# First-level products of the chunked recurrence scheduled six ticks behind their operands instead of three

## The chip, the cores and the metric

The kernel runs on one core of a Trainium2 chip. The metric is the device time of one execution in microseconds (us); lower is better. The engines are named as the profile names them: PE multiplies matrices, DVE works on vectors and reads the matmul results, ACT applies functions and copies, POOL adds and issues some transfers, SP issues most transfers.

## The reference

One layer of a hybrid encoder over 2048 rows of width 1024, in fp32. The part that the change touches is the gated linear recurrence (4 heads of 128), written chunk by chunk:

```python
def hgrn2_mixer(zq, zf, zi, zo, lb, norm_g):
    q = jax.nn.silu(heads(zq))
    f = lbh + (1.0 - lbh) * jax.nn.sigmoid(heads(zf))
    log_f = jnp.log(f)
    k = 1.0 - f
    v = heads(zi)
    ...
    def step(state, xs):
        qc, kc, vc, gc = xs
        b = jnp.cumsum(gc, axis=2)
        diff = b[:, :, :, None, :] - b[:, :, None, :, :]
        decay = jnp.exp(jnp.where(causal[:, :, None], diff, -jnp.inf))
        attn = jnp.einsum('bhtk,bhtsk,bhsk->bhts', qc, decay, kc)
        o = (jnp.einsum('bhts,bhsv->bhtv', attn, vc)
             + jnp.einsum('bhtk,bhkv->bhtv', qc * jnp.exp(b), state))
        ...
def reference(...):
    for l in range(DEPTH):
        xn = rmsnorm(x, norm1_g[l])
        z = xn @ w_in[l]
        ...
        ya = pool_mixer(u_pool, pool_w[l], pool_scale[l]) @ w_pa[l]
        yb = hgrn2_mixer(zq, zf, zi, zo, lower_bounds[l], hgrn_norm_g[l]) @ w_pb[l]
        merged = gates[:, :, 0] * ya + gates[:, :, 1] * yb
        x = x + merged @ w_o[l]
        x = x + conv_glu_ffn(rmsnorm(x, norm2_g[l]), w_up[l], conv_w[l], conv_b[l], w_down[l])
    return rmsnorm(x, final_g)
```

## The kernel before

**Tiling.** The rows go through in two passes of 1024, each of two halves of 512 columns (rows lie on the free axis). A pass is a mixer (the input projection, the pooling branch, the recurrence, two branch projections `pa` and `pb`, the output projection `wo`) and then a feed-forward part (`up`, `dn`). Each big product is made as seven block products, P1 to P7, by a scheme of the Strassen kind, over sums of blocks (`B11`, `T1`, ...), and each block product as three matmuls per tile, because an fp32 operand is split in a high and a low part (`ops`, lines 212 and 213 for the weights). A unit of the projection is 7 x 12 = 84 matmuls of 128x512, all recorded on line 147. The first pass also writes the sums of weight blocks that it makes (line 411) to DRAM (`kw...`, line 321), for the second pass.

**What sets the order.** The program is written as tasks (Python generators) that are stepped between matmuls. `mm` records one big matmul; every sixth is a *tick* (`MM_PER_TICK`), on which the next weights are converted and every task whose wait is over is stepped; `yield n` in a task means n ticks, which is 6n big matmuls. From this recording, a scheduler gives each engine a fixed order. A call of `in_turn(ins)` keeps the instruction behind the last big matmul recorded before it; all else may be moved. Each engine runs its own order strictly: an instruction that waits holds what is queued behind it on that engine.

**The recurrence.** `hgrn_task` runs for one head and one half of the rows; the projection units `fr` (forget logits and q), `ur` (pooling input) and `gr` (gates) are what the PE does meanwhile. When a unit `fr` is done, its two halves are queued, and two tasks run side by side. A task makes the 128x128 matrices of attention weights (`att`, shown as `at`) level by level, for pairs of blocks of 1, 2, 4 and 8, 16 and 32, and 64 rows. A level's product on PE (`pl`, lines 986, 946, 999) needs `ks` (k) and a form of q from DVE and ACT; DVE then copies the product into `att` under masks (lines 993, 1006, 954, 957) and multiplies decay into q, k and d (f) for the next level (lines 1012, 1014, 1016, 967 and others). After the levels come a transposition of k (`pk`), the state update (`pv` on PE, line 1029; `ss`, four steps on DVE, line 1037), the output (`po`, lines 1045 and 1047), its norm (ACT line 1052, POOL 649 and 650, DVE `ot` 1058) and a transposition (`pt`, line 1064).

The operands of the first level are q1, made on ACT (lines 903, 904) and DVE (line 905), and k (line 894). Between them and the product stands the `yield 3` on line 908. The other levels wait `AHEAD`, which is 3, in the same place.

**Buffers.** Nearly every 128x512 tile lies in one of 77 shared slots (`N_SLOTS`). A new tile takes a slot that an old one leaves; if the old one was being stored to DRAM, the first writer of the new tile waits for that store to land. Which slot a tile gets is settled with the order. The pooling branch (`pool_task`, sums `s` on line 854, `p` on line 859, `pm` on lines 867 to 869) and the gates (`gt`, line 1354, stored by line 876) draw on the same slots.

Of the kernel before, what the change touches and what calls it, by code (L numbers as in the profile page):

```python
# [70 lines left out]
AHEAD = 3  # L71
# [9 lines left out]
def tile_trunk(  # L81
# [803 lines left out]
    def hgrn_task(b, h, d, q, vd, zd, od):  # L885
# [19 lines left out]
        dve.tensor_tensor(q1[:, :, 0], qo, do, ALU.mult)  # L905
        dve.tensor_tensor(qe, qe, de, ALU.mult)
        dve.tensor_tensor(qo, q1[:, :, 0], de, ALU.mult)
        yield 3
        def mask(key, n):
            m = masks[key]  # L910
            return m.unsqueeze(1).to_broadcast([P, n, m.shape[1], m.shape[2]])
# [365 lines left out]
    def mixer(b0, forms, late):  # L1277
# [14 lines left out]
        def runner():  # L1292
            while taken[0] < 2 * HEADS:
                if queue:
                    taken[0] += 1
                    yield from hgrn_task(*queue.pop(0))
                else:
                    yield 1
# [487 lines left out]
```

## Time and profile before

| | us |
|---|---|
| median of 3 runs | 2555.31 |
| lowest, highest | 2554.01, 2557.34 |
| the profiled execution's own time | 2554.45 |
| its span (first to last instruction) | 2552.7 |
| PE idle over the span | 34.1 |
| of it before products of line 986, waiting for line 905 | 5.2 |

The page gives busy time by engine; PE idle is the span less its 2518.6 us busy. A timeline row has the start, the length, the engine, the line, the operation and the tiles; the bracket at its end is the idle time of the engine just before it and what ended that. A matmul of 128x512 is listed with about 0.4 us but the next starts 0.23 us after it, since they overlap. "PEclk" is the granted clock of PE as a share of full speed.

### The profile page before, as it was taken

To read this page: it belongs to the slowest core of one execution; us is meant where nothing else is said; L and a number is where in the kernel's file an instruction comes from. 1 tells how busy PE (TensorE), PEld (TensorE's weight loads), DVE (VectorE), ACT (ScalarE), POOL (GpSimd) and SP (SyncE) were. 2 spreads that over 40 slices of the span, in tenths; PEclk is the share of its full clock that TensorE was granted. 3 is DMA by queue.
4 is the path that set the end of the run, shared out by engine and by line. 5 is a ranking of instruction groups with operands and counts; after the bars stand their busy time and mean duration, and the time that the engine had idled before them with its cause. 6 is when DMAs were issued, how large, how long until landed. Compare 5 with 4: busy or idle time off the path is not lost.

```text
span 2552.7 us, 35665 instructions
## 1 busy us (share of the span) xinstructions
PE 2518.6 (99%) x11508; PEld 2058.3 (81%) x11508; DVE 1978.0 (77%) x3518; ACT 1176.0 (46%) x2218; POOL 753.4 (30%) x1117
## 2 busy tenths in 40 slices
PE   9999999999999999999999999999999999999998
PEld 7788877888788888888887888888887888888887
DVE  7798869588888787885585877675978888778755
ACT  6434434324545454554454343432355554545534
POOL 1344344002454334461230111200034433325410
PEclk9999999999999999999999999999999999999999
DMA  7777767768898879997444343446443544446952
GB/s 261 236 196 228 212 182 230 238 214 240 194 248 247 226 223 246 258 356 254 134 147 149 102 134 112 132 153 221 149 159 96 157 150 144 148 137 231 332 162 100
DMA packets 252332, 493.76 MB, mean 193 GB/s; under 512 B 26544, under 2 KB 43056, under 8 KB 251824
## 3 DMA queue, kind: packets, MB, share of 16 engines
q1 hardware_dynamic: 185664, 315.70, 39.2%
q0 software_dynamic: 41504, 110.64, 16.9%
q10 hardware_dynamic: 24976, 65.13, 7.4%
q8 instruction: 91, 1.49, 0.2%
q14 instruction: 97, 0.79, 0.1%
HBM read 381.79 MB, written 187.17 MB: 223 GB/s over the span
## 4 chain that ended last, share of the span: by engine, by line
PE 71%; DVE 1%; ACT 1%; issue 0%; POOL 0%; POOLq 0%; DVEq 0%; ACTq 0%
PE dn_P L147 16%; PE up_Z L147 14%; PE up_V L147 9%; PE up_X L147 9%; PE wo_P L147 3%; PE gr_Z L147 3%; PE gr_X L147 2%; PE pb L147 2%; PE gr_V L147 2%; PE pa L147 2%; PE fr_Z L147 1%; PE io_Z L147 1%; PE fr_X L147 1%; PE io_V L147 1%; PE fr_V L147 1%; PE pl L946 1%
## 5 line engine op out<-in xcount | busy, mean ns | idle before, releaser
L212 ACT CAST ops<-raw 128x512 fp32r<-128x512 f32 x736 | 454.3, 620 | 835.7 <-PE dn_P L147 176.2
L213 DVE TENSOR_TENSOR ops<-raw,ops 128x512 fp32r<-128x512 f32 x736 | 548.8, 749 | 208.3 <-ACT ops L212 203.0
L1522 DVE SCALAR_TENSOR_TENSOR e<-h,cols,e 128x512 f32<-128x512 f32 x176 | 143.1, 816 | 31.7 <-ACT e L1520 23.3
L1520 ACT ACTIVATE e<-h,cols 128x512 f32<-128x512 f32 x176 | 142.6, 814 | 24.9 <-DVE h L1079 18.6
L1525 DVE SCALAR_TENSOR_TENSOR e<-h,cols,e 128x512 f32<-128x512 f32 x176 | 134.0, 770 | 2.8
L881 POOL DMA_DIRECT2D g_P<-dg_P x154 | 85.1, 560 | 161.0 <-PE dn_P L147 116.0
L1186 POOL TENSOR_TENSOR gf_P<-e,e 128x512 f32<-128x512 f32 x44 | 61.1, 1389 | 149.2 <-DVE e L1531 95.7
L1317 POOL TENSOR_TENSOR q<-q,qs 128x512 f32<-128x512 f32 x16 | 21.8, 1364 | 199.5 <-ACT qs L1316 192.3
L1186 POOL TENSOR_TENSOR gf_P<-gf_P,e 128x512 f32<-128x512 f32 x44 | 59.2, 1345 | 72.2 <-DVE e L1531 71.7
L1515 POOL COPY h<-h 128x2 f32<-128x2 f32 x88 | 42.0, 489 | 114.0 <-DVE h L1078 109.9
L1529 ACT ACTIVATE e<-e 128x512 f32<-128x512 f32 x88 | 55.5, 631 | 38.6 <-DVE e L1525 38.3
L1517 POOL COPY hist<-h 128x2 f32<-128x2 f32 x88 | 36.0, 409 | 117.8 <-DVE h L1079 116.1
L1079 DVE TENSOR_TENSOR h<-up_u,up_V 128x512 f32<-128x512 f32 x88 | 60.1, 683 | 13.4 <-PE up_V L147 12.9
L1354 ACT ACTIVATE gt<-gt,cols 128x512 f32<-128x512 f32 x48 | 34.8, 725 | 75.9 <-DVE gt L1079 47.6
L1161 DVE TENSOR_TENSOR x<-x,wo_P 128x512 f32<-128x512 f32 x88 | 56.0, 681 | 12.2 <-PE wo_P L147 12.0
L1161 DVE TENSOR_TENSOR ac<-ac,dn_P 128x512 f32<-128x512 f32 x72 | 47.1, 682 | 16.5 <-PE dn_P L147 16.4
L1545 POOL DMA_DIRECT2D dg_P<-gf_P x88 | 51.4, 584 | 7.9 <-POOL gf_P L1186 7.2
L931 POOL COPY qm<-q 128x64 f32<-128x64 f32 x64 | 23.0, 377 | 100.7 <-DVE q L937 34.8
L1113 ACT COPY up_e<-up_X 128x512 f32<-128x512 f32 x44 | 25.8, 587 | 57.8 <-PE up_X L147 52.7
L946 PE MATMUL pl<-qm,k 128*128 128x192 f32 x256 | 50.3, 326 | 0.3 <-DVE qm L935 0.3
L1515 POOL COPY h<-hist 128x2 f32<-128x2 f32 x88 | 46.1, 531 | 7.7 <-DVE m_T42l L618 7.7
L946 PEld LDWEIGHTS pl<-qm,k 128*128 128x128 f32 x256 | 44.2, 189 | 5.1 <-issue 0.6
(1301 smaller groups left out, 8118.1 us busy)
## 6 DMA issues: line engine op xcount, KB each, us to landing
g_P<-dg_P POOLq DMA_DIRECT2D x154, 256.0 KB, 6.1
raw<-in_w_up_t SPq DMA_DIRECT2D x132, 256.0 KB, 3.1
raw<-in_w_in_t SPq DMA_DIRECT2D x98, 256.0 KB, 3.4
dg_P<-gf_P POOLq DMA_DIRECT2D x88, 256.0 KB, 4.0
dg_P<-e SPq DMA_DIRECT2D x66, 256.0 KB, 3.4
raw<-in_w_dn SPq DMA_DIRECT2D x66, 256.0 KB, 3.8
x<-in_x SPq DMA_DIRECT2D x64, 256.0 KB, 4.8
gd<-gt ACTq DMA_DIRECT2D x64, 256.0 KB, 3.6
```

What stands on the lines that cost most here:

```text
L147: count[1] = pe.matmul(*args, **kw)
L212: self.mark = act.copy(hi, v)
L213: low = self.low = dve.tensor_tensor(lo, v, f32(hi), ALU.subtract)
L881: eng.dma_start(t, d)
L946: ins = pe.matmul(pa_[:, c * 192 : c * 192 + 192], ks[:, (i + c) * P : (i + c + 1) * P], mv[:, c].rearrange("p s x -> p (s x)"), start=Tru ...
L1079: return dve.tensor_tensor(dst, t, ps, ALU.add if how == "add" else ALU.subtract)
L1161: dve.tensor_tensor(t, t, ps[j], ALU.add if sg > 0 else ALU.subtract)
L1186: pin(eng.tensor_tensor(t, x0, x1, op))
L1515: pool.tensor_copy(h[:, 0:2], hist[:, mt] if hf == 0 else hs[s, 0][:, TB : TB + 2])
L1520: in_turn(act.activation(t, h[:, 2:], AF.Identity, bias=col(o_cb + mt), scale=col(o_cw + 4 * MF + mt)))
L1522: in_turn(second(dve.scalar_tensor_tensor(t, h[:, 1 : 1 + TB], col(o_cw + 2 * MF + mt), t, ALU.mult, ALU.add)))
L1525: dve.scalar_tensor_tensor(t, h[:, 0:TB], col(o_cw + mt), t, ALU.mult, ALU.add)
```

## The change

The first level's products are recorded six ticks (36 big matmuls) behind their operands, where it was three (18). Every other wait keeps its number, and nothing else is edited; so all later steps of each task are recorded later too.

```diff
@@ -905,7 +905,7 @@
         dve.tensor_tensor(q1[:, :, 0], qo, do, ALU.mult)
         dve.tensor_tensor(qe, qe, de, ALU.mult)
         dve.tensor_tensor(qo, q1[:, :, 0], de, ALU.mult)
-        yield 3
+        yield 2 * AHEAD
         def mask(key, n):
             m = masks[key]
             return m.unsqueeze(1).to_broadcast([P, n, m.shape[1], m.shape[2]])
```

Every engine has the same instructions before and after; they are in another order, and tiles lie in other slots, in the two mixers alone.

**PE, the first pair of tasks of the first pass.** Before (`q_0_1492` and `q_0_1506` are the two halves' q1; the rows left out are the other big matmuls of the same units):

```order
L147 MATMUL gr_0_Z<-x_T23l,ops_1415 128x512
L147 MATMUL gr_0_Z<-x_T23h,ops_1415 128x512
L986 MATMUL pl_0_1_1539<-q_0_1492,k_0_1487 128x128 x4
L147 MATMUL gr_0_X<-x_f4h,ops_1481 128x512
...
L147 MATMUL gr_0_X<-x_f7h,ops_1481 128x512
L986 MATMUL pl_0_1_1544<-q_0_1506,k_0_1501 128x128 x4
L147 MATMUL gr_0_V<-x_T10h,ops_1434 128x512
```

And now:

```order
L147 MATMUL gr_0_Z<-x_T23h,ops_1415 128x512
L147 MATMUL gr_0_V<-x_T10h,ops_1434 128x512
...
L147 MATMUL gr_0_X<-x_f7h,ops_1481 128x512
L147 MATMUL gr_0_Z<-x_T30h,ops_1457 128x512
...
L986 MATMUL pl_0_1_1574<-q_0_1492,k_0_1487 128x128 x4
L986 MATMUL pl_0_1_1579<-q_0_1506,k_0_1501 128x128 x4
L147 MATMUL gr_0_Z<-x_T32h,ops_1457 128x512
...
L147 MATMUL gr_0_Z<-x_T43h,ops_1528 128x512
L986 MATMUL pl_0_2_1648<-q_0_1493,k_0_1487 128x128 x4
L986 MATMUL pl_0_2_1653<-q_0_1507,k_0_1501 128x128 x4
```

The first half's product stands 30 big matmuls later and the second's 18; both are at one place now, and the second level's products follow 18 big matmuls behind them, where it was 36 and 24. The same holds for the last pair of the first pass (30 later, second level 18 behind, before 24 and 36) and for these pairs of the second pass.

**DVE, behind the first state update of the first pass.** A bracket names the semaphores that the instruction waits for; DMAHW ones are those of transfers. Before:

```order
L1115 TENSOR_TENSOR fr_1_u_2063<-fr_1_e_2035,fr_1_Z 128x512 [waits DVE_49,PE_49]
L854 TENSOR_TENSOR s_1_2_2080<-s_1_1_1985 128x512 [waits DMAHW7_49,DMAHW1_49,Pool_49]
L1037 SCALAR_TENSOR_TENSOR ss_0_2095<-st_0_122,f_0_1424,pv_0_2090 128x128 [waits DMAHW7_49,PE_49]
L213 TENSOR_TENSOR ops_2075<-w56s_2072,ops_2075 128x512 [waits Activation_49]
L859 SCALAR_TENSOR_TENSOR p_0_2110<-s_0_1_2009,u_0_1993 128x512 [waits DVE_49]
```

And now:

```order
L213 TENSOR_TENSOR ops_2061<-w56s_2058,ops_2061 128x512 [waits Activation_49]
L213 TENSOR_TENSOR ops_2095<-raw_1732,ops_2095 128x512 [waits DMAHW1_49,Activation_49]
L854 TENSOR_TENSOR s_1_2_2080<-s_1_1_1977 128x512 [waits DMAHW7_49,DVE_49]
L859 SCALAR_TENSOR_TENSOR p_0_2098<-s_0_1_2009,u_0_1985 128x512 [waits DVE_49]
L618 TENSOR_TENSOR pl_0l<-p_0_2098,pl_0h 128x512 [waits DMAHW0_49,Activation_49]
L854 TENSOR_TENSOR s_1_2_2104<-s_1_1_2013 128x512 [waits PE_49]
L1119 TENSOR_TENSOR fr_1_u_2113<-fr_1_Z,fr_1_e_2021 128x512 [waits DVE_49]
L1079 TENSOR_TENSOR q_1_2115<-fr_1_u_2113,fr_1_V 128x512 [waits DVE_49,PE_49]
L1037 SCALAR_TENSOR_TENSOR ss_0_2142<-st_0_122,f_0_1424,pv_0_2137 128x128 [waits PE_49]
```

Before, the pooling sum `s_1_2` of line 854 took slots whose stores (DMAHW7, DMAHW1) had been issued 142 and 55 big matmuls earlier, and the state step followed at once. Now it takes the slot of `w56s`, a weight sum whose store to `kwfq1ins` (DMAHW7) is issued at the same place of the order; the state step stands six instructions behind it, and PE needs that step 27 big matmuls behind the `pv` products.

**DVE, the third head's state update in the first pass.** Before:

```order
L854 TENSOR_TENSOR s_3_2_3705<-s_3_1_3612 128x524 [waits DVE_49,PE_49]
L213 TENSOR_TENSOR ops_3732<-raw_3320,ops_3732 128x512 [waits DMAHW1_49,Activation_49]
L1037 SCALAR_TENSOR_TENSOR ss_2_3720<-st_0_126,f_2_2994,pv_2_3715 128x128 [waits DMAHW3_49,DVE_49]
L1037 SCALAR_TENSOR_TENSOR ss_2_3720<-ss_2_3720,f_2_2994,pv_2_3715 128x128 [waits DVE_49] x2
L1037 SCALAR_TENSOR_TENSOR st_1_127<-ss_2_3720,f_2_2994,pv_2_3715 128x128 [waits DVE_49]
```

And now:

```order
L854 TENSOR_TENSOR s_3_2_3694<-s_3_1_3586 128x524 [waits DMAHW2_49,DVE_49]
L854 TENSOR_TENSOR s_3_2_3718<-s_3_1_3627 128x524 [waits Pool_49]
L1119 TENSOR_TENSOR gr_4_u_3727<-gr_4_Z,gr_4_e_3643 128x512 [waits DVE_49,PE_49]
L1079 TENSOR_TENSOR gt_1_4_3729<-gr_4_u_3727,gr_4_V 128x512 [waits DMAHW3_49,DVE_49,PE_49]
L213 TENSOR_TENSOR ops_3746<-w100s_3743,ops_3746 128x512 [waits Activation_49]
L213 TENSOR_TENSOR ops_3781<-w100s_3740,ops_3781 128x512 [waits Activation_49]
L1037 SCALAR_TENSOR_TENSOR ss_2_3756<-st_0_126,f_2_2969,pv_2_3751 128x128 [waits DMAHW5_49,DVE_49,PE_49]
```

The state step now takes the slot of `w100s`, whose sum POOL makes once PE has passed the second half's `pk`, and whose store to `kwfq3ins` follows that sum; the products `po` that need the step stand 36 big matmuls behind that `pk`.

## The prediction

> **What bounds the kernel now.** I read the page first.
>
> ```profile
> span 2552.7 us, 35665 instructions
> ...
> PE 2518.6 (99%) x11508; PEld 2058.3 (81%) x11508; DVE 1978.0 (77%) x3518; ACT 1176.0 (46%) x2218; POOL 753.4 (30%) x1117
> ...
> PE 71%; DVE 1%; ACT 1%; issue 0%; POOL 0%; POOLq 0%; DVEq 0%; ACTq 0%
> ```
>
> PE is busy for 2518.6 of 2552.7 us, and the chain that ended last is PE for 71% and hardly anything else. So PE's own work sets the time, and a change that leaves every matmul in place can only alter what PE loses between them: 2552.7 - 2518.6 = 34.1 us. The list of who waited for whom on PE says what these are (total, times, longest):
>
> ```profile
> engine line waited for: us in total, times, longest us
> PE pl L986 <- DVE q L905: 5.2, 3, 2.3
> ...
> PE pt L1064 <- DVE ot L1058: 2.5, 2, 1.8
> PE gr_X L147 <- ACT gr_e L1113: 2.2, 2, 1.6
> ...
> PE pl L999 <- DVE k L967: 1.4, 2, 0.9
> PE pm L867 <- ACT pl_2h L617: 1.2, 1, 1.2
> ```
>
> The wait that the change is about is the first: 5.2 us in three waits for line 905, which makes q1. The other rows shown are waits inside the mixers, for steps that the change moves. The busy time by stretch shows where there is anything to lose (each engine's busy time with its count, then clock, DMA share and GB/s):
>
> ```profile
> core 0: us, PE busy (x) PEld busy (x) DVE busy (x) ACT busy (x) POOL busy (x), PEclk, DMA share, GB/s
> 110.00:560.00 450.00, 439.56 (x2148) 363.82 (x2147) 352.57 (x776) 161.42 (x358) 145.45 (x153) 0.99 0.74 216
> ...
> 1290.00:1720.00 430.00, 427.01 (x2131) 356.31 (x2130) 325.87 (x772) 188.12 (x401) 66.41 (x104) 1.00 0.44 133
> ```
>
> In the first mixer (110 to 560 us) PE is idle for 450.0 - 439.6 = 10.4 us, DVE is busy for 78% and the DMA engines for 74%; in the second (1290 to 1720 us) PE is idle for 3.0 us and the DMA share is 44%. What a moved step may newly run into is therefore in the first mixer.
>
> **Term 1, the three waits for line 905: -5.2 us.** The first of them, and DVE's row at it:
>
> ```profile
> 128.11 0.40 PE L147 MATMUL gr_Z<-x_T23h,ops 128*128 128x512 f32 x1
> 130.18 1.13 PE L986 MATMUL pl<-q,k 128*128 128x128 f32 x8 [1.67 <-DVE q L905]
> ...
> 131.38 0.39 PE L147 MATMUL gr_X<-x_f4l,ops 128*128 128x512 f32 x1
> ...
> 133.69 0.40 PE L147 MATMUL gr_X<-x_f7h,ops 128*128 128x512 f32 x1
> ```
>
> ```profile
> 129.62 0.41 DVE L905 TENSOR_TENSOR q<-q,f 128x256 f32<-128x256 f32 x1
> ...
> 131.42 0.41 DVE L905 TENSOR_TENSOR q<-q,f 128x256 f32<-128x256 f32 x1
> ```
>
> PE was free at 128.11 + 0.40 = 128.51 (by the pace of its matmuls at 128.34) and q1 of the first half was there at 129.62 + 0.41 = 130.03. From 131.38 to 133.69 ten matmuls start, so one costs 0.231 us. The product now comes 30 matmuls later: 128.34 + 30 x 0.231 = 135.3 us, 5.2 us after q1 of the first half and 3.5 us after that of the second (131.83). The same distance of 30 is there at the other two waits:
>
> ```profile
> 140.40 1.95 PE L986 MATMUL pl<-q,k 128*128 128x128 f32 x16
> ...
> 142.88 0.39 PE L147 MATMUL gr_Z<-x_T41h,ops 128*128 128x512 f32 x1
> ...
> 394.26 3.24 PE L986 MATMUL pl<-q,k 128*128 128x128 f32 x16 [2.29 <-DVE q L905]
> ...
> 398.43 0.39 PE L147 MATMUL gr_V<-x_T11h,ops 128*128 128x512 f32 x1
> ```
>
> ```profile
> 1401.03 1.13 PE L986 MATMUL pl<-q,k 128*128 128x128 f32 x8 [1.24 <-DVE q L905]
> 1403.80 0.50 PE L147 MATMUL gr_X<-x_f4h,ops 128*128 128x512 f32 x1 [1.64 <-ACT gr_e L1113]
> ```
>
> The waits there are 2.29 and 1.24 us; 30 matmuls are 6.9 us, so both vanish. 1.67 + 2.29 + 1.24 = 5.2 us. At 1403.80 a wait of 1.64 us for ACT's copy of the unit's first product (gr_e) follows. In the new order 12 other matmuls (2.8 us) stand ahead of that row in place of the wait and the product (1.24 + 0.8 us), but ACT's queue has one more conversion ahead of the copy; I leave the 1.64 us as it is.
>
> **Term 2, the clock behind the longest of them: -1.7 us.** The 16 products and three matmuls from 140.40 to 142.88 took 2.48 us. The same work from 394.26 to 398.43, behind the wait of 2.29 us, took 4.17 us. The difference is 1.69 us, and the stretch around it shows why:
>
> ```profile
> 391.00:398.00 7.00, 4.71 (x23) 4.12 (x22) 7.00 (x14) 5.10 (x12) 3.66 (x4) 0.77 0.99 265
> ```
>
> The granted clock was 0.77 there, against 0.99 over the mixer. Behind 1.67 us of waiting there is no such loss (131.38 to 133.69 is the usual pace). So the 2.29 us wait cost some 4 us, and this goes with it. [...]
>
> **Term 3, the third of the kind, k for the 64-row level: -1.4 us.**
>
> ```profile
> 433.62 0.65 PE L999 MATMUL pl<-q,k 128*64 128x64 f32 x8 [0.94 <-DVE k L967]
> ```
>
> This wait (0.94, and 0.4 for the other half; 1.4 in the list) comes 14 matmuls behind the 16-row products. In the new order the distance is 23, so PE arrives 9 x 0.231 = 2.1 us later on this clock, and 0.94 us is covered.
>
> **Term 4, the waits behind one held slot: -3.0 us.** In the first pass one stall of DVE is a slot whose store had not landed:
>
> ```profile
> 363.79 0.70 DVE L854 TENSOR_TENSOR s<-s 128x520 f32<-128x520 f32 x1 [4.90 <-DMA gd<-gt]
> ```
>
> ```profile
> 366.99 0.30 PE L1064 MATMUL pt<-ident,ot 128*128 128x128 f32 x1 [1.80 <-DVE ot L1058]
> ...
> 371.62 0.50 PE L867 MATMUL pm<-pl_2h,ops 128*128 128x512 f32 x1 [1.22 <-ACT pl_2h L617]
> ```
>
> DVE stood for 4.9 us at a pooling sum, what is queued behind it came late, and PE waited 1.80 us for the output of the third head and 1.22 us for a pooled half. In the new order that sum takes another slot and these two products stand 24 and 12 matmuls later (5.5 and 2.8 us), so I take both waits out.
>
> **Term 5, what the new slots cost: +5 us, between 0 and 10.5.** Slots are dealt anew, and two places look tight. How long a store takes is in the rows of the first mixer (count, KB, median us to landing), and in one row of ACT:
>
> ```profile
> gd<-gt ACTq DMA_DIRECT2D x32, 256.0 KB, 3.7
> ...
> kwfq3ins<-w100s SPq DMA_DIRECT2D x2, 256.0 KB, 9.0
> ...
> kwfq1ins<-w56s SPq DMA_DIRECT2D x1, 256.0 KB, 11.7
> ```
>
> ```profile
> 187.63 0.86 SPq L321 DMA_DIRECT2D kwfq1ins<-w56s  x1
> ...
> 199.44 0.69 ACT L871 ACTIVATE mx<-pm,cols 128x512 f32<-128x512 f32 x1 [6.34 <-DMA kwfq1ins<-w56s]
> ```
>
> The rows at the place of need and at the weight sum, from before:
>
> ```profile
> 184.66 1.63 POOL L411 TENSOR_TENSOR w56s<-w51s,raw 128x512 f32<-128x512 f32 x1 [5.25 <-ACT pl_0h L617]
> ...
> 199.06 0.39 PE L147 MATMUL fr_V<-x_B223h,ops 128*128 128x512 f32 x1
> ```
>
> Place B: DVE's pooling sum now waits for the store of w56s. Before, that store was issued at 187.63 and held ACT until 199.44. Less the 1.67 us gained by then it lands at 197.7; the sum and five more DVE operations of some 0.6 us stand ahead of the state step, which is then there at 197.7 + 3.7 = 201.4. The matmul of the second row is the one that stands at the need in the new order, 27 behind `pv`; PE came to it at 199.06, and now comes 1.67 us of waiting and some 0.8 us of small products sooner, at about 196.5. That is a wait of 4.9 us at most. But POOL's sum, which stood 5.25 us behind ACT's copy of `pl_0h`, waits for PE's `pk` alone in the new order, so the store may go out some 5 us sooner, and then the wait is 0. Place C: the state step of the third head waits for the store of w100s, 9.0 us, behind such a POOL sum (1.6 us), which starts only when PE is 36 matmuls (8.3 us) ahead of the need. With 0.3 us for the first step that is 1.6 + 9.0 + 0.3 - 8.3 = 2.6 us at most, and 0 if the store lands as quickly as the gates' (3.7 us). Elsewhere I allow what the one held slot of before cost, 0 to 3.0 us. Together 0 to 10.5; the rows lie on both sides of the middle, so I take 5. Below nothing it cannot be, since these waits were not there.
>
> What the change costs beside that: the second level's products now follow 18 matmuls (4.2 us) behind the first level's. In between DVE must copy and multiply k for both halves:
>
> ```profile
> L1006 DVE COPY_PREDICATED at<-m,pl 128x256 f32<-128x256 uint8 x32 | 24.5, 767 | 0.0
> ...
> L1014 DVE TENSOR_TENSOR k<-k,f 128x256 f32<-128x256 f32 x48 | 24.0, 500 | 0.0
> ...
> L993 DVE COPY_PREDICATED at<-md,pl 128x256 f32<-128x256 uint8 x32 | 23.5, 735 | 3.0 <-PE pl L986 3.0
> ```
>
> That is 2 x (0.74 + 0.77 + 0.50) = 4.0 us at these lengths. With the other half's eight product instructions (0.8 us) PE has 5.0 us of other work; I cost it at nothing, and it is a rival below. The tail is covered too: the last head's output comes 24 matmuls later, some 100 matmuls ahead of the first `pb` product.
>
> **The sum.** -5.2 - 1.7 - 1.4 - 3.0 + 5.0 = -6.3 us. On the profiled execution's 2554.45 us that is 2548.2; the median shown, 2555.31, lies 0.9 us above it, so 2549.0 us.
>
> **The rivals.** (1) *Slot holds win, slower.* The mechanism is term 5 alone: a held DVE instruction in the first pass makes PE wait for over 2 us, and each such wait takes the clock with it, 1.7 us as at 394.26. B at 4.9 + 1.7, C at 2.6 + 1.7 and 3.0 elsewhere are 13.9 us against gains of 11.3: 2557.9 us; with one more hold as long as the 4.9 us one and not covered by PE's work, 4.9 + 1.7 more: 2564.5. It decides from 11.3 us on. For it: a DMA share of 74%, stores of 9.0 and 11.7 us, and stores issued just ahead of their wait. Against it: 36 matmuls of cover at C, the earlier sum at B. (2) *The next level takes the wait.* DVE is held between the levels, as the 1.64 us and the 4.9 us rows show can be, and the second level's products wait up to 1.5 us at four places, 6 us: -6.3 + 6 gives 2555.0 us, no change; with half of it, 2552. For it: 18 matmuls in place of 24 to 36. Against: in the list of before PE never waited for line 1014 or 1006, at distances of 24 and more. (3) *All moved waits vanish and none comes*, -11.3: 2544.0 us. (4) *The change doesn't do what it says*, the scheduler having put the products back: 2555.3; the order of PE speaks against it.
>
> **How the numbers follow.** Forecast 0.45, around 2549 with a range of its own from 2545.5 to 2551.5. Slot holds 0.20, next level 0.19, all gains 0.13, nothing moved 0.03. A measurement of this kernel tells about 0.2%, 5.1 us, from no change: below 2550.2 is faster, above 2560.4 slower. Faster: 0.39 of the forecast's 0.45 and the 0.13, 0.52. Same: 0.06 of the forecast, the 0.19, 0.03 and 0.06 of the slot holds, 0.34. Slower: 0.14. For 8 in 10 the range leaves out the lower end of "all gains" and the slot holds above 2558: 2543 to 2558 us.
>
> **What would show it.** Right: no row "pl L986 <- q L905" among PE's waits, no clock of 0.77 in the first mixer, and a PE idle time of the second mixer of under 2 us. Term 5 shows as idle time of PE before `po` (line 1047) with a transfer as the cause on DVE. Wrong: a wait of PE at line 986 for k (line 1014) is rival 2; several waits over 2 us in the first mixer, each with a lower clock behind it, are rival 1. Idle time or clock lost outside the two mixers would make the whole account wrong, since nothing moves there.

## The result, and the profile after

| | before | after |
|---|---|---|
| median of 5 runs (us) | 2554.01 | 2567.69 |
| lowest, highest | 2550.76, 2557.34 | 2566.11, 2568.71 |
| span of the profiled execution | 2552.7 | 2566.0 |
| PE busy, PE idle in it | 2518.6, 34.1 | 2522.4, 43.6 |

The changed kernel takes 1.0055 times as long, with an interval from 1.0045 to 1.0066: slower by some 14 us, where 6.3 us less were forecast (2549.0 us) and at most 2558 us were allowed for. The page of the changed kernel, span and busy times:

```profile
span 2566.0 us, 35639 instructions
...
PE 2522.4 (98%) x11508; PEld 2058.8 (80%) x11508; DVE 1980.7 (77%) x3518; ACT 1177.3 (46%) x2218; POOL 741.2 (29%) x1117
```

The span grew by 13.3 us: 9.5 us are more idle time of PE (43.6 - 34.1), and 3.8 us are more busy time for the same instructions, which goes with a lower mean granted clock of PE (0.995 for 0.997). The list of PE's waits after the change (total, times, longest) shows what came and what went:

```profile
engine line waited for: us in total, times, longest us
PE gr_Z L147 <- DVE gr_u L1119: 10.3, 6, 3.5
PE gr_X L147 <- ACT gr_e L1113: 3.9, 2, 2.0
...
PE pv L1029 <- ACT kt L1022: 2.6, 1, 2.6
...
PE pt L1064 <- DVE ot L1058: 2.4, 1, 2.4
```

The waits for line 905 (5.2 us in three), for line 967 (1.4) and for `pl_2h` (1.2) are no longer in the list. In their place stands one that hardly was there before (0.5 us in two): PE waits in front of `gr_Z` for DVE's `gr_u`, line 1119, 10.3 us in six waits. Four of them are at the pairs (3.50, 1.59, 1.52 and 1.50 us), one of 1.75 us is at the second head. And it waits 2.6 us for `kt` and 2.4 us for the last `ot`.

To see where the 13.3 us lie I cut both executions at places up to which PE has run the same set of instructions, and compared the pieces (from the starts of PE's rows, times of before in brackets):

| piece of the program | before | after | difference |
|---|---|---|---|
| ahead of the first recurrence products (to 126) | 124.4 | 123.3 | -1.1 |
| first pair, to the products of the 4-row level (to 148) | 21.7 | 26.6 | +4.9 |
| from there (to 265) | 117.6 | 117.6 | -0.1 |
| from there (to 350) | 84.8 | 86.0 | +1.2 |
| third head's state update (to 391) | 41.2 | 42.9 | +1.7 |
| last pair (to 472) | 80.8 | 79.1 | -1.8 |
| first `pa` products (to 488) | 16.0 | 22.2 | +6.2 |
| second mixer, first pair (1396 to 1418) | 21.8 | 23.8 | +2.0 |
| second mixer, last pair (1652 to 1673) | 20.9 | 22.8 | +1.9 |
| the rest (to 2540) | 2009.3 | 2007.6 | -1.7 |

Three things carry the loss: three of the four pairs (the last pair of the first pass gained 1.8 us), the stretch of the `pa` products, and the third head's state update. One execution of each kernel is compared, and a piece differs by 1 to 2 us between executions with the same order in it: in the kernel `tail_pin` of experiment 6, which has the changed kernel's order up to the `pa` products, the first pair lost 3.9 us and the third head's state update 0.3 us.

**The pairs.** PE's and then DVE's rows at the first pair after the change:

```profile
134.63 1.95 PE L986 MATMUL pl<-q,k 128*128 128x128 f32 x16
...
141.48 0.80 PE L147 MATMUL gr_Z<-x_T40h,ops 128*128 128x512 f32 x1 [3.50 <-DVE gr_u L1119]
```

```profile
137.85 0.71 DVE L993 COPY_PREDICATED at<-md,pl 128x256 f32<-128x256 uint8 x1
138.37 0.76 DVE L1006 COPY_PREDICATED at<-m,pl 128x256 f32<-128x256 uint8 x1
138.93 0.45 DVE L1014 TENSOR_TENSOR k<-k,f 128x256 f32<-128x256 f32 x1
...
140.75 0.67 DVE L1119 TENSOR_TENSOR gr_u<-gr_Z,gr_e 128x512 f32<-128x512 f32 x1
```

The 16 first-level products of both halves now run at 134.63, six big matmuls ahead of the point where PE begins the next block product in bank `gr_Z` (a bank, in the kernel, is the place in which PE leaves a product until another engine has read it). Before PE may write that bank again, DVE must have read it; that read is line 1119, called u3 below. But in DVE's order the six instructions that work on the products (lines 993, 1006, 1014, twice; the second three are left out above) stand ahead of line 1119. DVE gets to it at 140.75, so PE waits 3.50 us. Before the change the same two instructions were here:

```profile
140.60 0.69 DVE L1119 TENSOR_TENSOR gr_u<-gr_Z,gr_e 128x512 f32<-128x512 f32 x1
```

```profile
142.10 0.47 PE L147 MATMUL gr_Z<-x_T40h,ops 128*128 128x512 f32 x1
```

DVE came to line 1119 at about the same time, 140.60, but PE only asked for it at 142.10: it had waited 1.67 us earlier and had 16 products of the second level (1.95 us) between the two block products. The change took the earlier wait away, moved these products behind the bank's turn, and so turned both into a later, longer wait. What it cost beyond its length is in the windows (the clock is the third figure from the end):

```profile
core 0: us, PE busy (x) PEld busy (x) DVE busy (x) ACT busy (x) POOL busy (x), PEclk, DMA share, GB/s
...
141.40:144.90 3.50, 3.42 (x8) 2.75 (x9) 0.71 (x2) 2.33 (x6) 0.41 (x2) 0.50 0.19 75
144.90:149.90 5.00, 5.00 (x27) 4.30 (x27) 2.90 (x6) 1.04 (x3) 2.14 (x3) 0.78 0.12 45
```

The granted clock was 0.50 for 3.5 us and 0.78 for the next 5 us, which is 1.75 + 1.1 = 2.9 us lost. With 3.50 - 1.67 us of waiting it makes 4.7 of the 4.9 us. In `tail_pin` the same wait of 3.50 us was followed by a clock of 0.67 for 3.5 us and 0.89 for 4.9 us, which is 1.7 us, so the wait repeats and the loss of clock behind it varies. In the second mixer DVE isn't full (busy for 13.1 of 20 us from 1405 to 1425), and the form is plainer:

```profile
1421.26 1.95 PE L986 MATMUL pl<-q,k 128*128 128x128 f32 x16
...
1426.08 0.51 PE L147 MATMUL gr_Z<-x_T40h,ops 128*128 128x512 f32 x1 [1.50 <-DVE gr_u L1119]
```

```profile
1422.41 0.73 DVE L993 COPY_PREDICATED at<-md,pl 128x256 f32<-128x256 uint8 x1 [1.26 <-PE pl L986]
...
1425.35 0.67 DVE L1119 TENSOR_TENSOR gr_u<-gr_Z,gr_e 128x512 f32<-128x512 f32 x1
```

DVE even waits for the products, copies them for 2.9 us, and reads `gr_Z` only then; PE waits 1.50 us. This is little more than the wait for line 905 that went (1.24 us). What makes the piece 2.0 us longer is mostly the clock behind the wait for `gr_e` ahead of it, which is 1.84 us where it was 1.64: 0.75 over 3.0 us and 0.64 over 2.7 us, 1.7 us lost, and before the change it was 1.00 there.

**The `pa` products.** ACT, DVE and PE at the end of the first mixer:

```profile
484.42 1.14 ACT L212 CAST ops<-raw 128x512 fp32r<-128x512 f32 x2 [2.42 <-PE pa L147]
485.47 0.27 ACT L1052 ACTIVATE sq<-po 128x128 f32<-128x128 f32 x1
```

```profile
485.07 0.69 DVE L213 TENSOR_TENSOR ops<-raw,ops 128x512 fp32r<-128x512 f32 x1 [2.27 <-ACT ops L212]
...
486.88 1.12 DVE L1058 SCALAR_TENSOR_TENSOR ot<-po,ro,z 128x128 f32<-128x128 f32 x4
```

```profile
487.28 0.33 PE L1064 MATMUL pt<-ident,ot 128*128 128x128 f32 x1 [2.43 <-DVE ot L1058]
```

The last head's `ot` stands in DVE's order behind two weight conversions (line 213). Their cast on ACT waited 2.42 us for PE to be done with earlier `pa` products (the operand buffer is theirs), so PE's transposition waits, through DVE and ACT, for PE's own work: 2.43 us.

**The third head.** This is the prediction's place C. The hold of DVE came as feared, but it reached PE by another path. DVE, POOL, ACT and PE:

```profile
363.49 0.35 DVE L1037 SCALAR_TENSOR_TENSOR ss<-st,f,pv 128x128 f32<-128x128 f32 x1 [4.16 <-DMA kwfq3ins<-w100s]
```

```profile
365.06 1.04 POOL L854 TENSOR_TENSOR s<-s 128x512 f32<-128x512 f32 x1 [7.71 <-DVE st L1037]
```

```profile
366.14 0.69 ACT L1354 ACTIVATE gt<-gr_X,cols 128x512 f32<-128x512 f32 x1 [7.61 <-POOL s L854]
...
367.22 0.58 ACT L1022 COPY kt<-pk 128x512 f32<-128x512 f32 x1 [0.40 <-ACT gt L1354]
```

```profile
367.86 1.16 PE L1029 MATMUL pv<-v,kt 128*128 128x128 f32 x8 [2.59 <-ACT kt L1022]
```

DVE's state step waits 4.16 us for the store of `w100s`. POOL's pooling sum stands behind it, ACT's gate `gt` behind that sum, and ACT's copy `kt`, which PE wants, behind the gate. The products `po`, which the prediction had looked at, waited 0.27 us; PE's 2.59 us are at `pv`.

### The profile page after: what moved, and what is told of

Its sections match the earlier page's. It is cut to its first block, busy times and chain, and to the rows that moved or that the text cites. A ratio compares the mean times of both kernels' runs of the same rounds, so it can differ in the third digit from the quotient of the medians.

```text
span 2566.0 us, 35639 instructions
## 1 busy us (share of the span) xinstructions
PE 2522.4 (98%) x11508; PEld 2058.8 (80%) x11508; DVE 1980.7 (77%) x3518; ACT 1177.3 (46%) x2218; POOL 741.2 (29%) x1117
## 4 chain that ended last, share of the span: by engine, by line
PE 82%; DVE 2%; ACT 1%; issue 1%; DMA 1%; POOL 0%; ACTq 0%; DVEq 0%; POOLq 0%
PE dn_P L147 16%; PE up_Z L147 14%; PE up_X L147 10%; PE up_V L147 9%; PE wo_P L147 6%; PE pb L147 3%; PE pa L147 3%; PE gr_Z L147 3%; PE gr_V L147 2%; PE gr_X L147 2%; PE fr_Z L147 2%; PE io_Z L147 1%; PE pl L946 1%; PE fr_X L147 1%; PE fr_V L147 1%; PE io_V L147 1%
```

## The experiments

Each was timed against the kernel before on the same chip; the medians of before were 2552.46 to 2553.86 us. The ratios are those of the timed runs, with 95% intervals. A *pin* below is an edit that ties one instruction behind another in its engine's order.

**1. The order at u3.** Theory A is that DVE's order costs the time; theory B that DVE is full and would cost it in any order. `second(...)` ties an instruction behind the u3 (or u2, line 1115) that was made last.

```diff
-                dve.copy_predicated(ad, masks[-1 - lv].to_broadcast([P, NT, 64]), pv4[:, :, 1])
+                second(dve.copy_predicated(ad, masks[-1 - lv].to_broadcast([P, NT, 64]), pv4[:, :, 1]))
...
-            dve.tensor_tensor(k3[:, :, 0, :], k3[:, :, 0, :],
-                              d3[:, :, 1, 0:1].to_broadcast(full), ALU.mult)
+            (id if lv else second)(dve.tensor_tensor(k3[:, :, 0, :], k3[:, :, 0, :],
+                              d3[:, :, 1, 0:1].to_broadcast(full), ALU.mult))
```

> The change as it is, but DVE's copies of a first-level product (line 993) and the product of k behind them (line 1014, first level) are held behind the unit's last-made u3 or u2 (lines 1119 and 1115). Theory A (the six DVE instructions of the two halves stand in DVE's order ahead of u3, and PE waits for u3 before it may write the bank Z again): the waits gr_Z <- gr_u, 10.3 us in six and 1.2 us in two, fall to under 4 us together, the clock behind the 3.5 us one comes back (some 3 us), the rest (tail of the first mixer, kt wait) stays: 2555 to 2560 us. Theory B (DVE is full in that stretch, so the time is lost wherever the copies stand): the wait moves to the next result of DVE, at the second level's products or at gt, and the time stays within 2564 to 2569 us.

Measured: 2557.41 us, 1.0014 [1.0005, 1.0022], 10 us less than without the pin. The pin puts u3 ahead of the six instructions; a few other instructions of PE, DVE and ACT moved with it. PE's waits and two of its rows:

```profile
PE gr_Z L147 <- DVE gr_u L1119: 4.0, 5, 0.9
```

```profile
138.85 0.50 PE L147 MATMUL gr_Z<-x_T40h,ops 128*128 128x512 f32 x1 [0.78 <-DVE gr_u L1119]
...
162.55 0.89 PE L946 MATMUL pl<-qm,k 128*128 128x192 f32 x4 [1.23 <-DVE qm L935]
```

The 3.50 us became 0.78 us, the three others at the pairs 0.78 or 0.87. With those for line 1115 (1.6 us) that is 5.6 us where I had expected under 4, but the time is in the range of theory A. A holds for the loss. For the gain at the first pair, B fits: against before, the stretch up to 166 us is not shorter but 0.6 us longer (41.0 for 40.4 us), since a wait of 1.23 us for DVE's `qm` follows. Before the change DVE was busy for 31.8 of 32 us there (DVE's busy time is the third):

```profile
126.00:158.00 32.00, 30.01 (x150) 25.03 (x149) 31.81 (x81) 13.17 (x30) 16.23 (x20) 1.00 0.90 253
```

So nothing was won at the first pair by waiting later; that a full DVE is why is my reading, which no run tests alone.

**2. How much each queued instruction counts.** The changed kernel's order on PE, with two of the six instructions left out at each pair. The kernel leaves out the attention weights of neighbouring positions.

```diff
-            if lv < 2:
+            if lv == 1:
                 dve.copy_predicated(av[:, :, :, 1, :], mask(hh, NT), pv4)
```

> The change as it is, without DVE's second copy of the first level's product (line 1006 at level 1), so that the attention weights of neighbouring positions are left out. Two of the six DVE instructions ahead of u3 go, 0.57 us apart each. Theory A (PE waits for u3 through DVE's queue, and each instruction in it counts in full): the waits for gr_u L1119 at the pairs fall by 1.1 us each, from 3.50 to 2.3 or 2.5, and from 1.52, 1.50 and 1.59 to 0.3 or 0.5; PE's order is the same there. Theory B (something else ends last, the product's own length or the copy of gr_X): they fall by less than 0.3 us.

Measured, in a single run, 2563.74 us. The wait at the first pair is now:

```profile
140.73 0.73 PE L147 MATMUL gr_Z<-x_T40h,ops 128*128 128x512 f32 x1 [2.36 <-DVE gr_u L1119]
```

3.50 - 2.36 = 1.14 us for two instructions that held DVE for 0.56 and 0.57 us (138.37 to 138.93, 139.81 to 140.38): they count in full. The three others fell from 1.52, 1.50 and 1.59 to 0.78, 0.78 and 0.88, the value of experiment 1: a floor I had not expected. The traces show what it is. DVE and PE at the second mixer's first pair in experiment 1, then PE and DVE before the change:

```profile
1414.42 0.69 DVE L1119 TENSOR_TENSOR gr_u<-gr_Z,gr_e 128x512 f32<-128x512 f32 x1 [3.53 <-PE gr_Z L147]
```

```profile
1415.17 0.50 PE L147 MATMUL gr_Z<-x_T40h,ops 128*128 128x512 f32 x1 [0.78 <-DVE gr_u L1119]
```

```profile
1413.16 1.95 PE L986 MATMUL pl<-q,k 128*128 128x128 f32 x16
```

```profile
1413.35 0.69 DVE L1119 TENSOR_TENSOR gr_u<-gr_Z,gr_e 128x512 f32<-128x512 f32 x1 [1.44 <-PE gr_Z L147]
```

Even with DVE idle and nothing ahead of it, u3 can only start when PE has finished the product in `gr_Z` and runs for 0.69 us; PE wants the bank at once, so it waits 0.78 us. Before, 16 products of the second level (1.95 us) ran on PE meanwhile and covered it.

**3. Other distances.**

```diff
-        yield 2 * AHEAD
+        yield 7
```

> Seven ticks in place of six: the pair's products stand directly ahead of the matmul that needs u3, and in DVE's order u3 stands ahead of the copies; everything later comes six matmuls later still. Theory A: no wait of PE for gr_u L1119 at the pairs (3.5, 1.5, 1.5, 1.6 us before), so the mixers are 8 to 10 us shorter there; the tail of the first mixer is no better than with six ticks (6.2 us) or 1 to 3 us worse: 2557 to 2562 us. Theory B: no better than six ticks, 2566 to 2572 us.

> Four ticks: the pair's two products stand 12 and 11 big matmuls later than with three, one ahead of and one behind the next block product, and the second level's at 14 to 26 matmuls. Theory A: the waits for line 905 are gone (12 matmuls are 2.8 us against 2.3 us) and only one half's copies stand ahead of u3, so no wait for it over 1 us: 2549 to 2554 us. Theory B: DVE is as full, PE loses as much as before the change: 2554 to 2558 us.

With seven ticks (2559.35 us; ratio 1.0009 [0.9999, 1.0020], that of the medians is 1.0021, and the twelve runs spread from 2547.44 to 2562.46) u3 stands ahead of the copies, and the pairs' waits for it are gone as theory A says. Other waits came, the first of them:

```profile
PE pl L946 <- DVE k L967: 4.9, 2, 4.5
```

With four (`yield 4`; 2563.16 us, 1.0030 [1.0018, 1.0042]) both theories missed. The waits for line 905 and, at the pairs, for u3 are gone, but these came:

```profile
PE ur_Z L147 <- DVE ur_u L1119: 3.9, 2, 2.7
PE pl L986 <- DVE k L1014: 3.8, 2, 1.9
```

Here the second level's products, still early, wait for `k` of line 1014: my second rival, in another kernel than the one I had it for. So each distance removes the wait it is aimed at, and none gains. With three ticks in the first pass and seven in the second (`yield 7 if b >= 2 else AHEAD`):

> Three ticks in the first pass, seven in the second, no pin. By the stretches of seven_ticks the second mixer gains 1.4 us at its first pair and nothing elsewhere, and the first mixer is as before: 2551 to 2553.5 us, no change that can be told. Rival (tiles dealt anew late in the first pass cost there): 2555 us and over.

2554.03 us, 0.9999 [0.9990, 1.0008]: no change, as expected, though 0.5 us above the range, and the second mixer's first pair gained nothing. PE waited 1.0 us less there, but from 1394 to 1430 us the program took 36.1 us for 35.9: behind the wait of 1.84 us for `gr_e` the clock was 0.69 for 2.9 us and 0.73 for 3.0 us.

**4. Which heads.**

```diff
-        yield 2 * AHEAD
+        yield 2 * AHEAD if h < 3 else AHEAD
```

> Six ticks for the heads 0 to 2, three for the last head. Theory A with the tail (the last head's norm and output come so late that they fall between the branch product's weight conversions): the 6.2 us that the stretch before the pa products took more are gone, the waits at 403 and 412 us and the one at 1680 us too, while the 2.3 us wait for line 905 with its clock comes back: 2559 to 2562 us. Rival (the tail's loss comes from slots dealt anew, not from the lateness): the tail's waits stay or move, 2564 us and over.

2559.31 us, 1.0020 [1.0012, 1.0029]: as theory A has it, the stretch of the `pa` products took 15.9 us again. The middle heads alone (`yield AHEAD if h in (0, 3) else 2 * AHEAD`):

> Six ticks for heads 1 and 2 alone, three for heads 0 and 3, where two halves go together. By the stretches of the changed kernel the middle heads gain 1.3 us at 205 to 265 us, and lose 1.3 and 1.7 us behind it (u3, and the held slot with kt): 2553 to 2556 us. So heads 0 and 3 would be what costs the change over 10 of its 13.5 us. Rival (the loss belongs to the middle heads and what follows from them): 2560 us and over.

2561.16 us, 1.0028 [1.0017, 1.0040]. My expectation missed, the rival held: these heads cost some 7 us by themselves, with the wait for `kt` (2.6 us) and with waits for `ot` behind the middle heads (1.03 us at 297.20, 0.85 us at 1568.00) that the changed kernel has not. So the stretches don't add over kernels; the order around every moved step is dealt again.

**5. The held slot.** The state steps take no slot of their own.

```diff
-        ss = slot(f"ss{b}_{h}")
+        ss = kt
```

> The change as it is, but the state steps ss are written into the tile kt (each chunk of it is dead once its pv product has run), so that they take no slot and wait for no store. Theory C (the third head's state step waits 4.2 us for the store of w100s; POOL's pooling sum, ACT's gate and ACT's copy kt stand behind it, and PE waits 2.6 us at pv and loses some clock): this wait of DVE, the 2.6 us and the 0.3 us at po go, 2563 to 2566 us. Rival (only the slot moves, another tile of the same stretch waits for that store): 2566 to 2569 us.

2559.65 us, 1.0024 [1.0015, 1.0034]: 8 us less, far more than theory C allows. The hold is gone and the wait for `kt` fell from 2.59 to 1.29 us, but most of the gain was that the `pa` products no longer waited (49.0 us for 56.4 over the 200 big matmuls there; 49.1 before the change), though the last head is as late. DVE there:

```profile
480.58 1.12 DVE L1058 SCALAR_TENSOR_TENSOR ot<-po,ro,z 128x128 f32<-128x128 f32 x4
...
482.81 0.69 DVE L213 TENSOR_TENSOR ops<-raw,ops 128x512 fp32r<-128x512 f32 x1
```

Here `ot` stands ahead of the conversion (line 213).

**6. The end of the mixer.** In three more kernels the wait at the end of the mixer did not follow the lateness of the last head: the pin of experiment 1 with three ticks, with three for the last head only, and the latter with the state in `kt`.

> The kernel before (three ticks) with the pin of DVE's copies alone. If the pin helps only because the later products had come to stand ahead of u3 (theory A), it is worth little here, as PE never waited for u3 at the pairs before: 2552 to 2557 us. Rival (the pin is a gain of its own, so pin_copies says nothing on the change): 2545 to 2549 us.

> The copies behind u3 (as in pin_copies), and three ticks for the last head. Theory A with the tail, added up over the stretches: 2557.4 less 4.4 us in the stretch of the pa products and 1.1 us in the last pair of the second pass, with 1.2 us more where the last pair of the first pass waits for line 905 again: 2552 to 2555 us. Rival (the two gains are the same time counted twice): 2557 us and over.

> All three edits: copies behind u3, three ticks for the last head, the state steps in kt. If the three losses found (queue at u3, tail, held slot) are all that the change costs, what is left is its gain in the middle heads (2 us) and nothing at the first pair: 2549 to 2552 us. Rival: the slots dealt anew cost as much elsewhere, 2553 us and over.

The pin alone gives 2555.03 us, 1.0002 [0.9993, 1.0011]: no gain of its own. The others give 2557.26 us, 1.0013 [1.0004, 1.0022], and 2558.16 us, 1.0022 [1.0013, 1.0031]; both expectations missed, and the times are in the ranges of their rivals. In all three the last head has as few ticks as before the change, and `pt` waits 1.8 us (in the last 6.2 us, with `ot` behind a product `ya` that waits for a reloaded gate). The rows of the first, DVE and PE:

```profile
480.83 1.29 DVE L213 TENSOR_TENSOR ops<-raw,ops 128x512 fp32r<-128x512 f32 x2 [3.08 <-ACT ops L212]
482.04 1.12 DVE L1058 SCALAR_TENSOR_TENSOR ot<-po,ro,z 128x128 f32<-128x128 f32 x4
```

```profile
482.44 0.33 PE L1064 MATMUL pt<-ident,ot 128*128 128x128 f32 x1 [1.83 <-DVE ot L1058]
```

Again `ot` stands behind conversions. So the theory that the last head comes too late fell, and this one took its place: what counts is whether `ot` stands behind a conversion that waits for PE. The next edit, `tail_pin`, moves only that; in the changed kernel it puts two conversions of DVE behind `ot` and its neighbours, and leaves every other engine's order.

```diff
+            low = self.low = dve.tensor_tensor(lo, v, f32(hi), ALU.subtract); last_ot[0] and behind(low, last_ot[0])
...
+                                     ALU.mult, ALU.mult); last_ot[0] = ins if h == 3 and b % 2 == 0 else last_ot[0]
```

> The change as it is; the one thing moved in any engine's order is that two weight conversions of DVE (line 213) stand behind the last head's ot of the first half instead of ahead of it, in the stretch of the pa products of the first pass. Theory D (the tail's loss is DVE's order there: ot stands behind conversions whose cast waits until PE is done with earlier pa products, so PE waits for its own work): the 2.4 us wait of pt goes with the clock behind it, the stretch takes 3.5 to 5.5 us less: 2562 to 2564.5 us. Rival (the last head is simply too late, ot cannot be had sooner): pt waits within 0.5 us of before, 2566 to 2569 us.

2561.23 us, 1.0032 [1.0020, 1.0044], 0.8 us under the range. `pt` waits no more, the stretch takes 17.6 us for 22.2, as theory D says, and what is left there is a wait of `pa`:

```profile
PE pa L147 <- ACT mxs_2h L617: 1.1, 1, 1.1
```

Putting `pt` later instead (`yield 6` for the 4 ahead of `pt`, with the pin of experiment 1):

> The pin of pin_copies, and the last transposition pt two ticks further behind ot (six for four). Theory on the tail (ot stands in DVE's order behind weight conversions, whose cast waits until PE is done with the pa products before; 12 more matmuls on PE, 2.8 us, cover the 2.4 us): the wait of pt at the end of the first mixer goes with its clock, 2553 to 2555 us. Rival (the conversions wait for PE itself, so what is late moves along with it; or ot's order is dealt anew): pt or pa still wait over 1.5 us there, 2556 to 2559 us.

2557.81 us, 1.0017 [1.0008, 1.0027]: the expectation missed. The wait of `pt` went and the stretch was as before the change (16.9 us in both, cut 1 us later than in the table), but the time came no lower than with the pin alone: in the order dealt anew the wait for `kt` was 4.5 us.

**7. All together.**

> The copies behind u3 (pin_copies) and the two conversions behind ot (tail_pin). If the two losses are separate, 2557.4 less 3 to 5 us: 2552.5 to 2554.5 us, about the time before the change. Rival (they are the same time): 2556 us and over.

> Both pins, and the state steps in the tile kt. If the held slot of the third head is the third separate loss (2 to 3 us in its stretch): 2549 to 2552 us. Rival (slots dealt anew cost as much elsewhere, as in pin_three_kt): 2553 to 2557 us.

| the change with | ratio to before | interval |
|---|---|---|
| nothing else | 1.0055 | 1.0045 to 1.0066 |
| copies behind u3 | 1.0014 | 1.0005 to 1.0022 |
| conversions behind `ot` | 1.0032 | 1.0020 to 1.0044 |
| both | 1.0008 | 0.9999 to 1.0017 |
| both, and the state in `kt` | 1.0001 | 0.9992 to 1.0010 |

Both pins give 2556.03 us, 1.5 us above what I expected and at the rival's edge: alone they take off 4.1 and 2.3 thousandths, together 4.7 and not 6.4. Some of it is that the pin at u3 alone had taken 1.9 us off the stretch of the `pa` products already. With the held slot gone as well it is 2553.14 us, above the 2549 to 2552 us expected and in the rival's range, but no longer to be told from the time before the change. So the two pins take off most of what the change costs, and the three edits together all of it; the last step is not clear of the noise by itself (the intervals overlap). Nothing tried was faster than the kernel before.

## Why the prediction was wrong

**What held.** All three waits for line 905 went, as term 1 said (5.2 us), and those of term 3 (1.4 us) and term 4 (1.8 and 1.2 us). No second-level product waited, as I had costed it. Term 5 came out near its size: place C cost 0.27 us at `po`, 2.59 us at `pv` and 1.7 us by a clock of 0.70 and 0.79 over the 7 us behind it, 4.6 us for the 5. That is luck in part, since the prediction looked for the wait at `po` and it came at `pv`, through POOL and ACT. At place B DVE was held 4.25 us and PE didn't wait for the state step, as the lower bound had it:

```profile
193.91 0.69 DVE L854 TENSOR_TENSOR s<-s 128x512 f32<-128x512 f32 x1 [4.25 <-DMA kwfq1ins<-w56s]
```

**What failed is the sentence "I cost it at nothing" on DVE's work behind the moved products.** I set 4.0 us of DVE (its six instructions held it for 2.9 us) against the next thing of the recurrence, the second level's products, 18 matmuls on. The first instruction that was late was none of the recurrence: it was u3, which stands behind that work in DVE's order and which PE needs six matmuls on. Before the change the second-level products stood just ahead of that point and covered u3; I counted where they went, not what they left bare. That turned terms 1 and 2 around: the waits for line 905 were worth nothing at the first pair (41.0 us for 40.4 even with the pin), and three pairs lost 8.8 us (4.9, 2.0 and 1.9), of which 1.7 us are the clock behind the wait for `gr_e` that the prediction left as it was. At the last pair of the first pass the 2.29 us and the 1.7 us of clock of term 2 were saved, but waits of 2.05 us for `gr_e` and 1.52 us for u3 took their place, and what the pair gained, 1.8 us, is mostly term 3. Behind the 3.50 us wait 2.9 us of clock were lost, more than term 2 had in it.

**"The tail is covered too"** was wrong by 6.2 us. I counted the matmuls between the last output and the first `pb` product, but not what stands on DVE and ACT ahead of `ot`; moving two conversions behind `ot` took 4.6 us off that stretch.

The rivals were too narrow: none reached 2567.7 us. The first, slower by held slots, was on the right side at 2557.9 to 2564.5 us, but held slots were the smaller part of the loss; the second, a wait taking the other's place, had the right mechanism at the wrong instruction. What I named as its sign, a wait at line 986 for line 1014, only appears with four ticks.

Open stays the rest of why the two pins don't add, and what decides how much clock a wait costs.

## What to carry to other kernels

When a step is moved later on PE, look at what the other engines' fixed orders now hold behind that step's results, above all the reads that free a bank for PE's own next product; here they had only six matmuls of slack. Asking later for a result of a full engine may win nothing, as at the first pair here (41.0 us for 40.4): compare the time at which that engine reaches the next thing PE needs, before and after. And products that are moved away uncover whatever they had hidden at their old place, here a wait of 0.78 us behind 1.95 us of products.

## What the runs showed of the hardware

The clock did not follow the length of a wait alone. In the changed kernel it fell to 0.50 behind 3.50 us, but also to 0.64 behind one of 1.84 us (at 1415.42), and stayed at 1.00 behind one of 2.05 us (at 403.41):

```profile
403.30:406.00 2.70, 2.59 (x11) 2.15 (x12) 2.70 (x7) 1.41 (x5) 0.00 (x0) 1.00 1.00 156
1418.30:1421.00 2.70, 2.70 (x9) 2.19 (x8) 1.22 (x3) 0.62 (x1) 0.00 (x0) 0.64 0.00 0
```

The order doesn't decide it either. The kernels of experiment 1 and with both pins have the same order on every engine at the second mixer's first pair, and the same wait for `gr_e` (1.84 and 1.85 us); behind it, first in the one and then in the other:

```profile
1405.10:1408.10 3.00, 2.88 (x10) 2.29 (x11) 2.90 (x9) 0.50 (x2) 0.32 (x1) 0.76 0.43 150
```

```profile
1405.30:1408.30 3.00, 2.87 (x12) 2.36 (x13) 2.90 (x9) 0.50 (x2) 0.31 (x1) 1.00 0.46 150
```

In the 2.9 us that follow it is 0.66 and 1.00. What decides it stays open: the loss, some 1.7 us, came in the one execution and not in the other. The 0.77 that term 2 rests on was read in one execution of the kernel before (391 to 398 us).

And a short DVE multiplication took 1.38 us at a time when POOL's sum of two tiles ran, 0.39 us just before it, first DVE, then POOL:

```profile
134.60 0.39 DVE L1016 TENSOR_TENSOR f<-f 128x128 f32<-128x128 f32 x1
...
136.56 1.38 DVE L1016 TENSOR_TENSOR f<-f 128x128 f32<-128x128 f32 x1
```

```profile
135.82 1.87 POOL L411 TENSOR_TENSOR w44s<-w44s,raw 128x512 f32<-128x512 f32 x1 [7.04 <-PE pl L986]
```

This 1 us stood in the queue ahead of the 3.50 us wait as well. In this trace the other 15 multiplications of this form took 0.41 us or less, and none of them ran beside such a sum of POOL; in experiment 1's trace the one that did took 1.37 us. Of the same line's multiplications of 128x256 two ran beside such a sum and took 1.21 and 1.40 us (at 215.32 and 221.68), the others 0.43 us or less. So in this trace the slow ones ran beside POOL's sums. Before the change one of 128x256 beside such a sum (at 132.09) took 0.41 us; and no run here takes the sum away, so that it causes them is not shown.
